# Four edits where the up projection hands over to the down projection: order of small loads, PSUM reads, DRAM copies and late operands

## The chip, the cores and the metric

The kernel runs on one core of a Trainium2 chip. The metric is device time: microseconds of one execution on that core, as the median over several executions. TensorE does the matrix products, VectorE and ScalarE the elementwise work, SyncE issues most of the DMA transfers, ScalarE a few, and GpSimd the DMA transfers that accumulate in DRAM.

## The reference, cut to what matters

One residual block on a sequence of 512 rows with D_MODEL = 2048 and D_FF = 5632, all in float32. The change lies in the second half, from `h2` on, and in one of the six vectors of `mod`, `gt2`.

```python
mod = silu(c) @ w_ada + b_ada                      # (1, 6*2048)
sh1, sc1, gt1, sh2, sc2, gt2 = split(mod, 6)
h = modulate(rms_norm(x, g_mix), sh1, sc1)
mix = concat(rms_norm(rglru(h @ w_in[...])), rms_norm(attention(h @ w_in[...])))
x = x + gt1 * (mix @ w_out)                        # called x1 below
h2 = modulate(rms_norm(x, g_ffn), sh2, sc2)
gate, up = split(h2 @ w_up, 2)                     # each (512, 5632)
x = x + gt2 * ((silu(gate) * up) @ w_down)         # w_down: (5632, 2048)
```

## The kernel before, in words

Every float32 operand is split into a high and a low part, and each product is three TensorE products (high by high, high by low, low by high). ScalarE writes the high part (L221, L228) and VectorE subtracts it from the operand for the low part (L222, L229). In the trace's names `h` and `l` at the end of a tile's name are these parts.

**The up projection.** Its 44 feature tiles of 128 features come one after another (`for f in range(2 * STD, FT)`); the first four are done plainly, the 40 others (f = 4 to 43) by a scheme with seven half-size products in place of eight. Each of the 40 takes two weight chunks `uq_0r` and `uq_1r` of 1 MB (`fast_chunk`, L1025 to L1050): VectorE forms sums of blocks in place (L1043, L1044, L1047), and seven pairs of parts with the endings `a`, `c`, `s` and `t` come out. The two chunks lie in the buffers with the tags "raw" (chunk 0) and "raw2" (chunk 1). The results of a tile stand in four PSUM banks `uf{f}p`. VectorE and ScalarE read them in six instructions, L1079 to L1084, into `ug`, `uu` and `uw`; L1085 and L1086 make silu(gate) * up, and `keep_act` (L955 to L968) forms the sums that the down projection needs and writes them to DRAM as `td`.

**The down projection** has four phases (`PHASES`), again with seven products of blocks: 4 and 5, then 1 and 7, then 6, then 2 and 3. Each phase runs over 11 weight chunks q. A chunk (`dn_chunk`) loads `dq_{q}r` of 1 MB per product, through the same "raw" and "raw2" buffers, loads the activation parts `dq_{q}tl` from `td` (L1108), splits them (L1109, L1110), and splits the weights. The second product of phase 0 adds the first weights to its own (L1115). Two of the phases read weight sums from DRAM, `s2d` and `s4d`; these sums are built during the up projection by `sums24`: two copies of 1 MB on SyncE's queue, then accumulating DMA transfers on GpSimd's queue (L976).

**The vector gt2** is a dot product of `silu(c)` with 2048 columns of `w_ada`. It is formed during the up projection in 64 pieces, one per chunk from the 16th chunk on (`GT2_AT`): a load of 256 KB issued by ScalarE's queue (L173) and one VectorE instruction that multiplies and sums (L183). The 64 pieces share two buffers. After the last piece four small additions make `mod` (L187 to L189), and `gt2_spread` writes `mod` to DRAM as `gt2d` (L1145, on SyncE's queue) and reads it back spread over all partitions as `gt2b` (L1149). `gt2b` and `x1` are operands of the last step, `finish` (L1152).

**What sets the order.** A scheduler orders each engine's instructions by priority, which is the place in the program unless `tc.high_priority(offset=...)` raises it: weight loads and splits by AHEAD = 2000, some PSUM reads by EVAC = 2500. `tc.issue_after` holds a transfer back until a named instruction has been issued. Each engine then runs its list strictly in order. Its transfers are issued in the order of that list, too.

Of the kernel before, what the change touches and what calls it, by code (L numbers as in the profile page):

```python
# [10 lines left out]
AF = mybir.ActivationFunctionType  # L11
# [6 lines left out]
KT = D // P  # L18
# [5 lines left out]
FT = DFF // P  # L24
# [14 lines left out]
EVAC = 2500  # L39
# [25 lines left out]
def block_kernel(ctx, tc, xT, crow, adaT, vecs, bfr, w1, wyr, wqkv0, wqkv, wgate, wout, wup0, wups, wdn, outT):  # L65
    nc = tc.nc
# [32 lines left out]
    with tc.high_priority(offset=100000):  # L99
# [6 lines left out]
        for q in (2, 3):  # L106
            cs = slice(q * 512, (q + 1) * 512)
# [62 lines left out]
    def gt2_load(n):  # L170
        t = cp.tile([P, S], F32, name=f"gt2_{n}", tag="ssq", bufs=2)
        with tc.issue_after(tail_hi[-1]):
            nc.scalar.dma_start(out=t, in_=adaT[GT2 * KT + n // 4, :, (n % 4) * S:(n % 4 + 1) * S])  # L173
        gt2_src[n] = t

    def gt2_piece(n):
        if n == 0:
            gt2_load(0)
        if n < 4 * KT - 1:
            gt2_load(n + 1)  # L180
        t = gt2_src.pop(n)
        r = n % 4
        nc.vector.scalar_tensor_tensor(out=t, in0=t, scalar=1.0, in1=c_b[:, r * S:(r + 1) * S], op0=ALU.mult, op1=ALU.mult,  # L183
                                       accum_out=gt2_acc[:, r, n // 4:n // 4 + 1])
        if n == 4 * KT - 1:
            m = mods[GT2]
            nc.vector.tensor_add(m, gt2_acc[:, 0, :], vec[:, V_BADA + GT2 * KT:V_BADA + (GT2 + 1) * KT])  # L187
            for r in range(1, 4):
                nc.vector.tensor_add(m, m, gt2_acc[:, r, :])  # L189
# [175 lines left out]
    for kt in range(KT):  # L365
        if kt < 2:
            with tc.high_priority(offset=90000):
                xt, raws = w1_loads(kt)
        else:
            xt, raws = w1_loads(kt)  # L370
        a = cp.tile([P, 1], F32, name=f"A{kt}")
# [10 lines left out]
        for i in range(2):  # L382
            cs = slice(i * 512, (i + 1) * 512)
# [594 lines left out]
    def sums24(q, n):  # L978
        if n == 0:
            with tc.issue_after(up_loads[-1]):  # L980
                nc.sync.dma_start(out=s2d[q], in_=wdn[0, q])
                nc.sync.dma_start(out=s4d[q], in_=wdn[1, q])
        elif n < 3:
            dram_sum(s2d[q], wdn[n + 1, q])
        else:
            dram_sum(s4d[q], s2d[q])
# [69 lines left out]
    for f in range(2 * STD, FT):  # L1056
# [19 lines left out]
        w1_, w2_ = (ap_.tile([P, S], F32, tag="x", name=f"uw{f}_{i}", bufs=2) for i in range(2))  # L1076
        two = lambda t: t.rearrange("p (a b) -> p a b", a=2)
        twice = lambda t: t.unsqueeze(1).broadcast_to(halves)
        nc.scalar.activation(w1_[:, lo_half], m[1], AF.Copy)  # L1079
        nc.vector.tensor_add(two(g), two(ps[0]), twice(w1_[:, lo_half]))  # L1080
        nc.vector.tensor_sub(two(w2_), twice(g[:, hi_half]), two(ps[1]))
        nc.vector.tensor_add(g[:, hi_half], m[3], w2_[:, lo_half])  # L1082
        nc.vector.tensor_sub(u[:, lo_half], m[4], w2_[:, hi_half])
        nc.vector.tensor_sub(u[:, hi_half], m[5], w2_[:, hi_half])  # L1084
# [66 lines left out]

    def finish(y, tt, a, nm, out=True):  # L1152
        xt = page(nm + "x", "d")
        nc.sync.dma_start(out=xt, in_=x1t[tt, a])
        nc.vector.tensor_mul(y, y, gt2b[a])
        nc.vector.tensor_add(y, y, xt)
        if out:
            nc.gpsimd.dma_start(out=outT[tt][:, a * S:(a + 1) * S], in_=y)
# [125 lines left out]
```

## Time and profile before

| quantity | value |
|---|---|
| time, median of 3 executions | 2105.34 us (2105.25 to 2111.82) |
| the profiled execution | 2106.22 us, of which its span is 2104.5 us |
| granted TensorE clock, mean of the span | 0.993 |
| TensorE busy | 2046.4 us, 97% of the span |
| VectorE busy | 1707.3 us, 81% |
| ScalarE busy | 942.3 us, 45% |
| GpSimd busy | 92.2 us, 4% |

The span runs from the first to the last recorded activity; 1.72 us lie around it. Busy means that an instruction of that engine was running; the issuing of transfers isn't counted. In the trace a row with `[8.47 <-DVE ug L1080]` tells that the engine stood idle for 8.47 us just before the row, and that the VectorE instruction of line 1080 which wrote `ug` released it. PE is TensorE, DVE VectorE, ACT ScalarE, POOL GpSimd; SPq and ACTq are the transfers that SyncE and ScalarE issue. Granted clock is the share of full TensorE speed that the throttle gave in a stretch.

By time the kernel is: the first input product from 10 to 200 us, attention and the recurrent group to 600, the output projection to 760, the first four feature tiles to 850, the 40 tiles of the fast scheme to 1660.8 (20.2 us each), and the down phases to 1795, 1915, 1964 and 2100 us.

### The profile page before, as it was taken

To read this page: it belongs to the slowest core of one execution; us is meant where nothing else is said; L and a number is where in the kernel's file an instruction comes from. 1 tells how busy PE (TensorE), PEld (TensorE's weight loads), DVE (VectorE), ACT (ScalarE), POOL (GpSimd) and SP (SyncE) were. 2 spreads that over 40 slices of the span, in tenths; PEclk is the share of its full clock that TensorE was granted. 3 is DMA by queue.
4 is the path that set the end of the run, shared out by engine and by line. 5 is a ranking of instruction groups with operands and counts; after the bars stand their busy time and mean duration, and the time that the engine had idled before them with its cause. 6 is when DMAs were issued, how large, how long until landed. Compare 5 with 4: busy or idle time off the path is not lost.

```text
span 2104.5 us, 32286 instructions
## 1 busy us (share of the span) xinstructions
PE 2046.4 (97%) x12529; PEld 1856.7 (88%) x12529; DVE 1707.3 (81%) x2547; ACT 942.3 (45%) x1331; POOL 92.2 (4%) x111
## 2 busy tenths in 40 slices
PE   8999999999999999999999999999999899999999
PEld 6889898888788887999999999999999778888877
DVE  8999768887785569988798888888888777776785
ACT  4433447765433355444343333344434345545443
POOL 0000000100100000000000000000000000000000
PEclk9999999999999999999999999999999999999999
DMA  9989866667677532438877878888877677677784
GB/s 336 345 292 315 254 204 220 221 214 253 231 243 264 182 129 92 132 130 236 226 228 229 237 216 256 250 245 235 240 232 208 188 254 250 233 243 252 260 298 148
DMA packets 168412, 485.21 MB, mean 231 GB/s; under 512 B 20033, under 2 KB 45025, under 8 KB 163810
## 3 DMA queue, kind: packets, MB, share of 16 engines
q1 hardware_dynamic: 148898, 429.66, 59.9%
q0 software_dynamic: 10144, 36.70, 9.7%
q10 hardware_dynamic: 9216, 16.78, 2.4%
q8 instruction: 98, 1.61, 0.3%
q14 instruction: 56, 0.46, 0.1%
HBM read 447.40 MB, written 93.35 MB: 257 GB/s over the span
## 4 chain that ended last, share of the span: by engine, by line
PE 74%; DVE 12%; DMA 9%; issue 2%; ACT 2%; POOL 1%; SPq 0%; DVEq 0%; ACTq 0%
PE w1p L233 4%; PE dn7p L233 3%; PE dn1p L233 3%; DMA gt<-in_adaT 2%; PE dn5p L233 2%; PE dn6p L233 2%; PE yr1p L233 2%; PE up0p L233 2%; PE wo2p L233 2%; PE wo3p L233 2%; PE wo1p L233 2%; PE dn4p L233 2%; PE yr0p L233 2%; PE wo0p L233 2%; PE h3p L233 2%
## 5 line engine op out<-in xcount | busy, mean ns | idle before, releaser
L154 DVE SCALAR_TENSOR_TENSOR ada<-ada,c_b 128x1024 f32<-128x1024 f32 x96 | 116.0, 1219 | 26.8 <-DMA ada<-in_adaT 26.7
L228 ACT ACTIVATE uq_0sh<-uq_0r 128x1024 fp32r<-128x1024 f32 x40 | 42.4, 1060 | 208.3 <-DVE uq_0r L1044 183.6
L183 DVE SCALAR_TENSOR_TENSOR gt<-gt,c_b 128x512 f32<-128x512 f32 x64 | 43.9, 686 | 60.5 <-DMA gt<-in_adaT 60.5
L228 ACT ACTIVATE uq_1sh<-uq_1r 128x1024 fp32r<-128x1024 f32 x40 | 42.5, 1061 | 109.2 <-DVE uq_1r L1044 98.0
L976 POOL DMA_DIRECT2D s2d<-in_wdn x44 | 36.7, 909 | 685.0 <-DMA s2d<-in_wdn 676.8
L228 ACT ACTIVATE uq_0ah<-uq_0r 128x1024 fp32r<-128x1024 f32 x40 | 42.3, 1058 | 48.2 <-DMA td<-tw 3.6
L229 DVE TENSOR_TENSOR uq_0sl<-uq_0r,uq_0sh 128x1024 fp32r<-128x1024 f32 x40 | 49.0, 1226 | 18.1 <-ACT uq_0sh L228 18.1
L229 DVE TENSOR_TENSOR uq_0tl<-uq_0r,uq_0th 128x1024 fp32r<-128x1024 f32 x40 | 48.8, 1220 | 8.4 <-ACT uq_0th L228 8.4
L229 DVE TENSOR_TENSOR uq_0al<-uq_0r,uq_0ah 128x1024 fp32r<-128x1024 f32 x40 | 48.8, 1221 | 8.4 <-ACT uq_0ah L228 8.3
L233 PE MATMUL w1p<-hph,w1h 128*128 128x512 f32 x128 | 47.5, 400 | 6.1 <-ACT hph L377 6.1
L228 ACT ACTIVATE uq_1ah<-uq_1r 128x1024 fp32r<-128x1024 f32 x40 | 42.3, 1057 | 22.4 <-issue 11.9
L233 PE MATMUL w1p<-hpl,w1h 128*128 128x512 f32 x128 | 51.2, 400 | 0.0
L233 PE MATMUL w1p<-hph,w1l 128*128 128x512 f32 x128 | 50.8, 397 | 0.0
L229 DVE TENSOR_TENSOR uq_1tl<-uq_1r,uq_1th 128x1024 fp32r<-128x1024 f32 x40 | 48.8, 1219 | 2.0 <-ACT uq_1th L228 2.0
L1085 ACT ACTIVATE ug<-ug 128x512 f32<-128x512 f32 x40 | 25.3, 633 | 53.5 <-DVE ug L1082 53.5
L1043 DVE TENSOR_TENSOR uq_0r<-uq_0r 128x1024 f32<-128x1024 f32 x40 | 48.7, 1217 | 0.0
L229 DVE TENSOR_TENSOR uq_1sl<-uq_1r,uq_1sh 128x1024 fp32r<-128x1024 f32 x40 | 48.7, 1217 | 0.0
L229 DVE TENSOR_TENSOR uq_1al<-uq_1r,uq_1ah 128x1024 fp32r<-128x1024 f32 x40 | 48.6, 1215 | 0.0
L1043 DVE TENSOR_TENSOR uq_1r<-uq_1r 128x1024 f32<-128x1024 f32 x40 | 48.6, 1214 | 0.0
L228 ACT ACTIVATE uq_0th<-uq_0r 128x1024 fp32r<-128x1024 f32 x40 | 41.9, 1048 | 12.4 <-DVE uq_0r L1047 2.6
L228 ACT ACTIVATE uq_1th<-uq_1r 128x1024 fp32r<-128x1024 f32 x40 | 42.0, 1051 | 10.5 <-PE uf36p L1066 1.3
L164 DVE SCALAR_TENSOR_TENSOR ada<-ada,c_b 128x1024 f32<-128x1024 f32 x32 | 39.0, 1220 | 1.7 <-DMA ada<-in_adaT 1.7
(12770 smaller groups left out, 8149.0 us busy)
## 6 DMA issues: line engine op xcount, KB each, us to landing
ada<-in_adaT SPq DMA_DIRECT2D x128, 512.0 KB, 5.1
uq_1r<-in_wups SPq DMA_DIRECT2D x80, 512.0 KB, 7.5
uq_0r<-in_wups SPq DMA_DIRECT2D x80, 512.0 KB, 5.0
s2d<-in_wdn POOLq DMA_DIRECT2D x44, 512.0 KB, 9.3
adf<-in_adaT SPq DMA_DIRECT2D x32, 512.0 KB, 6.0
gt<-in_adaT ACTq DMA_DIRECT2D x64, 256.0 KB, 4.7
s4d<-s2d POOLq DMA_DIRECT2D x22, 512.0 KB, 9.2
x<-in_xT SPq DMA_DIRECT2D x32, 256.0 KB, 5.6
```

The lines of the kernel that those rows point to most:

```text
L154: nc.vector.scalar_tensor_tensor(out=t, in0=t, scalar=1.0, in1=cs, op0=ALU.mult, op1=ALU.mult, accum_out=ac)
L164: nc.vector.scalar_tensor_tensor(out=t, in0=t, scalar=1.0, in1=c_b[:, cs], op0=ALU.mult, op1=ALU.mult, accum_out=ada_acc[j][:, hf, i:i + 1])
L183: nc.vector.scalar_tensor_tensor(out=t, in0=t, scalar=1.0, in1=c_b[:, r * S:(r + 1) * S], op0=ALU.mult, op1=ALU.mult, accum_out=gt2_acc[:, ...
L228: tail_hi.append(nc.scalar.activation(R(hi[:, :n]), raw_ap, AF.Copy).ins)
L229: tail_lo.append(nc.vector.tensor_sub(R(lo[:, :n]), raw_ap, hi[:, :n]).ins)
L233: nc.tensor.matmul(ps, lhsT=R(l), rhs=R(r), start=start, stop=stop)
L976: nc.gpsimd.dma_start(out=out[:, cs], in_=src[:, cs], accum_op=ALU.add)
L1043: nc.vector.tensor_add(blocks[:, 0:3:2], blocks[:, 0:2], blocks[:, 2:3].broadcast_to([P, 2, 512]))
L1085: nc.scalar.activation(g, g, AF.Silu)
```

## The change

There are four edits.

1. `gt2_piece`: pieces 0 and 1 are loaded at the start, and piece n+2 is loaded after piece n's VectorE instruction; before, piece n+1 was loaded ahead of piece n's instruction. There are still two buffers.
2. `sums24`: each of the two 1 MB copies from DRAM to DRAM is cut in two, over the columns, so that a row of a copy is 1024 floats; there are four transfers per weight chunk instead of two.
3. The six PSUM reads of a feature tile stand in a `high_priority` block, with the offset EVAC for the last tile (f = 43) and 0 for the others.
4. `finish`: its load of `x1` is held back until the last load but one that has been noted in `dn_loads`, the list of down weight loads, has been issued.

```diff
     def gt2_piece(n):
         if n == 0:
             gt2_load(0)
-        if n < 4 * KT - 1:
-            gt2_load(n + 1)
+            gt2_load(1)
         t = gt2_src.pop(n)
         r = n % 4
         nc.vector.scalar_tensor_tensor(out=t, in0=t, scalar=1.0, in1=c_b[:, r * S:(r + 1) * S], op0=ALU.mult, op1=ALU.mult,
                                        accum_out=gt2_acc[:, r, n // 4:n // 4 + 1])
+        if n < 4 * KT - 2:
+            gt2_load(n + 2)
...
             with tc.issue_after(up_loads[-1]):
-                nc.sync.dma_start(out=s2d[q], in_=wdn[0, q])
-                nc.sync.dma_start(out=s4d[q], in_=wdn[1, q])
+                for i in range(2):
+                    cs = slice(i * 1024, (i + 1) * 1024)
+                    nc.sync.dma_start(out=s2d[q][:, cs], in_=wdn[0, q, :, cs])
+                    nc.sync.dma_start(out=s4d[q][:, cs], in_=wdn[1, q, :, cs])
...
-        nc.scalar.activation(w1_[:, lo_half], m[1], AF.Copy)
-        nc.vector.tensor_add(two(g), two(ps[0]), twice(w1_[:, lo_half]))
...
+        with tc.high_priority(offset=EVAC if f == FT - 1 else 0):
+            nc.scalar.activation(w1_[:, lo_half], m[1], AF.Copy)
+            nc.vector.tensor_add(two(g), two(ps[0]), twice(w1_[:, lo_half]))
...
-            nc.sync.dma_start(out=raw[:, i * 1024:(i + 1) * 1024], in_=src[:, i * 1024:(i + 1) * 1024])
+            ld = nc.sync.dma_start(out=raw[:, i * 1024:(i + 1) * 1024], in_=src[:, i * 1024:(i + 1) * 1024])
+        dn_loads.append(ld.ins)
...
         xt = page(nm + "x", "d")
-        nc.sync.dma_start(out=xt, in_=x1t[tt, a])
+        with tc.issue_after(dn_loads[-2]):
+            nc.sync.dma_start(out=xt, in_=x1t[tt, a])
```

The rows of TensorE and GpSimd stand as before but for one swapped pair of matmuls. On the other engines the lists change at three places that the prediction speaks of. In the rows below a number behind a name tells one buffer or piece from another; the line numbers of the changed kernel are some higher than those of the kernel before.

VectorE, from the end of the last up tile into the first down chunk. `uf43p` are the PSUM banks of the last up tile, `dq_0` is the first down chunk. Before:

```order
L229 TENSOR_TENSOR uq_1tl<-uq_1r,uq_1th 128x1024
L1110 TENSOR_TENSOR dq_0tl<-dq_0tl,dq_0th 128x512
L183 SCALAR_TENSOR_TENSOR gt_63_17107,gt_acc<-gt_63_17107,c_b 128x512
L189 TENSOR_TENSOR mod_127<-mod_127,gt_acc 128x16
L229 TENSOR_TENSOR dq_0w0l<-dq_0r,dq_0w0h 128x1024
L1110 TENSOR_TENSOR dq_1tl<-dq_1tl,dq_1th 128x512
L1115 TENSOR_TENSOR dq_1r<-dq_1r 128x2048
L229 TENSOR_TENSOR dq_0w1l<-dq_0r,dq_0w1h 128x1024
L1110 TENSOR_TENSOR dq_1tl<-dq_1tl,dq_1th 128x512
L229 TENSOR_TENSOR dq_0w0l<-dq_0r,dq_0w0h 128x1024
L1110 TENSOR_TENSOR dq_2tl<-dq_2tl,dq_2th 128x512
L1080 TENSOR_TENSOR ug_17221<-uf43p_16997,uw_0_17223 128x512
```

With the change:

```order
L230 TENSOR_TENSOR uq_1tl<-uq_1r,uq_1th 128x1024
L1117 TENSOR_TENSOR dq_0tl<-dq_0tl,dq_0th 128x512
L230 TENSOR_TENSOR dq_0w0l<-dq_0r,dq_0w0h 128x1024
L1117 TENSOR_TENSOR dq_1tl<-dq_1tl,dq_1th 128x512
L1122 TENSOR_TENSOR dq_1r<-dq_1r 128x2048
L230 TENSOR_TENSOR dq_0w1l<-dq_0r,dq_0w1h 128x1024
L1117 TENSOR_TENSOR dq_1tl<-dq_1tl,dq_1th 128x512
L1084 TENSOR_TENSOR ug_17243<-uf43p_17021,uw_0_17245 128x512
L230 TENSOR_TENSOR dq_0w0l<-dq_0r,dq_0w0h 128x1024
L1085 TENSOR_TENSOR uw_1_17246<-ug_17243,uf43p_17022 128x512
L1117 TENSOR_TENSOR dq_2tl<-dq_2tl,dq_2th 128x512
L1086 TENSOR_TENSOR ug_17243<-uf43p_17023,uw_1_17246 128x256
```

The first read of the last tile's banks (`ug`, L1080, now L1084) has moved ahead of the second `dq_0w0l` and of the first `dq_2tl`. Piece 63 of gt2 and the last addition to `mod` have left this stretch: they now stand some twenty rows earlier, behind `uq_1tl` of tile 42 and ahead of `uq_0al` of tile 43.

SyncE's queue over the same stretch. Before:

```order
L1108 DMA dq_0tl<-td_0_6717 128x512
L1154 DMA f210x<-x1t_0_6572 128x512
L1096 DMA dq_1r<-in_wdn 128x1024 x2
L1108 DMA dq_0tl<-td_0_6717 128x512
L1154 DMA f220x<-x1t_2_6592 128x512
L965 DMA td_10_6738<-ug_16985 128x256
L1108 DMA dq_1tl<-td_1_6718 128x512
L1096 DMA dq_1r<-in_wdn 128x1024 x2
L1108 DMA dq_1tl<-td_1_6718 128x512
L1145 DMA gt2d<-mod_127 128x16x1
L1154 DMA f120x<-x1t_2_5960 128x512
L1154 DMA f110x<-x1t_0_5940 128x512
```

With the change:

```order
L1152 DMA gt2d<-mod_127 128x16x1
L1115 DMA dq_0tl<-td_0_6717 128x512
L1100 DMA dq_1r<-in_wdn 128x1024 x2
L1115 DMA dq_0tl<-td_0_6717 128x512
L1115 DMA dq_1tl<-td_1_6718 128x512
L966 DMA td_10_6738<-ug_17009 128x256
L1100 DMA dq_1r<-in_wdn 128x1024 x2
L1115 DMA dq_1tl<-td_1_6718 128x512
L1115 DMA dq_2tl<-td_2_6719 128x512
L1100 DMA dq_2r<-in_wdn 128x1024 x2
```

The transfer `gt2d` now stands ahead of the first `dq_0tl`; it stood behind the second `dq_1tl`. The four loads of `x1` with the names `f210x`, `f220x`, `f120x` and `f110x` are gone from here: they now stand near the end of the third phase, around `dq_10r<-s2d` and ahead of `dq_0r<-s4d`. The twelve other loads of `x1` stand where they stood.

ScalarE in feature tile 13, where the early pieces of gt2 are loaded. Before:

```order
L228 ACTIVATE uq_1th<-uq_1r 128x1024
L228 ACTIVATE uq_0ah<-uq_0r 128x1024
L173 DMA gt_2_9715<-in_adaT 128x512
L1040 ACTIVATE uq_1ch<-uq_1r 128x512
L228 ACTIVATE uq_0sh<-uq_0r 128x1024
```

With the change:

```order
L229 ACTIVATE uq_1th<-uq_1r 128x1024
L173 DMA gt_2_9609<-in_adaT 128x512
L229 ACTIVATE uq_0ah<-uq_0r 128x1024
L173 DMA gt_3_9720<-in_adaT 128x512
L1043 ACTIVATE uq_1ch<-uq_1r 128x512
```

Each load stands one place earlier, and so does its use on VectorE: piece 2 was used between `uq_0r` (L1043) and `uq_0r` (L1044), and is now used between the second and the third of these additions; piece 3 is now used two rows later, ahead of `uq_0tl`. From there on the same two places take turns to the end: a load behind `uq_0th` is used behind `uq_1sl` or `uq_1tl`, a load behind `uq_1th` is used behind `uq_1tl`, in both kernels, with the piece's number one higher in the changed one.

More of the change, by code (lines that the diff above doesn't have):

```diff
@@ L1078, in block_kernel @@
         twice = lambda t: t.unsqueeze(1).broadcast_to(halves)
-        nc.scalar.activation(w1_[:, lo_half], m[1], AF.Copy)
[L1080 to L1084, printed above, removed]
+        with tc.high_priority(offset=EVAC if f == FT - 1 else 0):
+            nc.scalar.activation(w1_[:, lo_half], m[1], AF.Copy)
+            nc.vector.tensor_add(two(g), two(ps[0]), twice(w1_[:, lo_half]))
+            nc.vector.tensor_sub(two(w2_), twice(g[:, hi_half]), two(ps[1]))
+            nc.vector.tensor_add(g[:, hi_half], m[3], w2_[:, lo_half])
+            nc.vector.tensor_sub(u[:, lo_half], m[4], w2_[:, hi_half])
+            nc.vector.tensor_sub(u[:, hi_half], m[5], w2_[:, hi_half])
         nc.scalar.activation(g, g, AF.Silu)
@@ L1095, in dn_load @@
         for i in range(2):
-            nc.sync.dma_start(out=raw[:, i * 1024:(i + 1) * 1024], in_=src[:, i * 1024:(i + 1) * 1024])
+            ld = nc.sync.dma_start(out=raw[:, i * 1024:(i + 1) * 1024], in_=src[:, i * 1024:(i + 1) * 1024])
+        dn_loads.append(ld.ins)
         return raw
+    dn_loads = []
     def dn_chunk(ph, q, hold=False):
```

## The prediction

> **What bounds the kernel now.** I read the busy times first, then what TensorE waits for, then the stretch with the longest wait.
>
> ```profile
> PE 2046.4 (97%) x12529; PEld 1856.7 (88%) x12529; DVE 1707.3 (81%) x2547; ACT 942.3 (45%) x1331; POOL 92.2 (4%) x111
> PE dn5p L233 <- DVE ug L1080: 8.5, 1, 8.5
> ```
>
> TensorE is busy for all but 58.1 us of 2104.5, and none of its matmuls goes away. So an edit can gain only where TensorE waits. The second line, from the view of waits, names the largest single wait of the last third: the first product of `dn5p` waits for the VectorE read of the last up tile's banks. TensorE's own rows give the place, and the chain of work says what was late there:
>
> ```profile
> 1675.87 0.76 PE L233 MATMUL dn5p<-dq_0w0h,dq_0th 128*128 128x512 f32 x1 [8.47 <-DVE ug L1080]
> 1678.06 0.77 PE L233 MATMUL dn5p<-dq_0w0h,dq_0th 128*128 128x512 f32 x1 [0.57 <-DVE ug L1082]
> ...
> 1641.10 19.70 PE uf43p L1066 x164
> 1661.80 11.94 DMA dq_2tl<-td
> 1674.43 0.69 DVE dq_2tl L1110
> 1675.12 0.61 DVE ug L1080
> 1678.06 6.47 PE dn5p L233 x21
> 1684.53 5.45 PE dn4p L233 x24
> ```
>
> The banks were full at 1660.79 (1641.10 plus 19.70). `ug` came at 1675.12 because it stands on VectorE behind `dq_2tl`, which waited for a load that took 11.94 us. The first chunk of `dn4p` and `dn5p` would take twice 5.45 us, to 1671.7, and ended at 1684.53: 12.8 us are lost here. Why the load was slow stands in the view of windows (here the last two columns, the busy share of the DMA engines and GB/s) and in the DMA table (KB and median us to landing):
>
> ```profile
> 1655.00:1660.00 5.00, 5.00 (x44) 5.00 (x43) 2.60 (x6) 1.78 (x3) 0.00 (x0) 1.00 0.92 270
> 1660.00:1665.00 5.00, 4.66 (x26) 3.74 (x25) 3.43 (x2) 0.00 (x0) 0.00 (x0) 1.00 0.52 14
> 1665.00:1670.00 5.00, 2.40 (x10) 1.60 (x9) 1.92 (x2) 1.85 (x3) 0.00 (x0) 1.00 0.60 35
> ...
> gt2d<-mod SPq DMA_DIRECT2D x1, 8.0 KB, 14.1
> f120x<-x1t SPq DMA_DIRECT2D x1, 256.0 KB, 15.4
> f110x<-x1t SPq DMA_DIRECT2D x1, 256.0 KB, 11.7
> dq_1r<-in_wdn SPq DMA_DIRECT2D x4, 512.0 KB, 4.9
> ```
>
> For 10 us the engines are more than half busy and move 14 to 35 GB/s. The one transfer of that shape in flight is `gt2d`: 2048 single floats, 8 KB, 14.1 us. Its issue and those behind it:
>
> ```profile
> 1643.89 0.33 SPq L1108 DMA_DIRECT2D dq_0tl<-td  x1
> 1655.92 0.38 SPq L1145 DMA_DIRECT2D gt2d<-mod  x1
> 1656.40 4.60 SPq L1154 DMA_DIRECT2D f120x<-x1t  x1
> 1661.42 0.32 SPq L1154 DMA_DIRECT2D f110x<-x1t  x1
> ```
>
> `gt2d` landed at 1670.0; `f110x`, issued 5.5 us behind it, at 1673.1, and `dq_2tl` at 1673.7. Whatever is issued behind `gt2d` lands some 3.1 to 3.7 us after it.
>
> **The handover with the change.** Two edits meet here. The PSUM reads no longer stand behind `dq_2tl`, and `gt2d` moves. In VectorE's new order the last addition to `mod` stands where this row stood, so `gt2d` is issued at about 1639, 17 us earlier, and directly ahead of the first `dq_0tl`, whose issue (1643.89) waits for TensorE to free its page and doesn't move. The slow stretch therefore goes from 1660 back to 1639. What it now holds up is in these VectorE and ScalarE rows:
>
> ```profile
> 1638.68 0.16 DVE L189 TENSOR_TENSOR mod<-mod,gt_acc 128x16 f32<-128x16 f32 x1
> 1649.38 0.69 DVE L1110 TENSOR_TENSOR dq_0tl<-dq_0tl,dq_0th 128x512 fp32r<-128x512 f32 x1
> 1652.12 1.22 DVE L229 TENSOR_TENSOR uq_1sl<-uq_1r,uq_1sh 128x1024 fp32r<-128x1024 f32 x1
> 1653.25 1.22 DVE L229 TENSOR_TENSOR uq_1tl<-uq_1r,uq_1th 128x1024 fp32r<-128x1024 f32 x1
> 1661.32 2.29 DVE L1115 TENSOR_TENSOR dq_1r<-dq_1r 128x2048 f32<-128x2048 f32 x1 [3.69 <-DMA dq_1r<-in_wdn]
> ...
> 1647.44 0.61 ACT L1109 ACTIVATE dq_0th<-dq_0tl 128x512 fp32r<-128x512 f32 x1
> ```
>
> Call T the landing of that `dq_0tl`. On ScalarE `dq_0th` stands ahead of `uq_1sh`, on VectorE `dq_0tl` ahead of `uq_1sl`, which TensorE needs for tile 43. From T to the end of `uq_1sl` it is 0.61 for `dq_0th` and the 3.96 from 1649.38 to 1653.34, so T + 4.6. TensorE needs it at 1655.3: the second chunk of the tile starts 84 matmuls of 0.12 us before 1660.79, and the pair stands 38 matmuls behind that. So TensorE stalls by T less 1650.7.
>
> T follows from how long `gt2d` alone blocks: at least the 10 us of the slow windows (to 1649), at most its 14.1 us (to 1653.1) with the 3.1 us behind (1656.2). I take the middle, T = 1652.6, since 1.35 MB (270 GB/s for 5 us) still went ahead of `gt2d` before and little does now. Then:
>
> - tile 43 ends 1.9 us late, at 1662.7; `uq_1tl` ends at T + 6.3 (with 0.6 for the `ug` now between the two) = 1658.9 and frees the buffer of `dq_1r`;
> - `dq_1r` lands 4.9 us later, 1663.8; the addition takes 2.29, `dq_0w1l` 1.22, so 1667.3; the second half of `dn4p` waits 1.9 us for it and ends at 1670.0;
> - behind it on VectorE `dq_1tl` 0.69, `ug` 0.69, `dq_0w0l` 1.22, `uw` 0.69, `dq_2tl` 0.69, three short reads of 0.42: the last bank is free at 1672.5. `dn5p` begins at 1670 to 1672.5 and, with 5.45 us, ends at 1677.9 at the latest.
>
> Against 1684.53 that gains **6.6 us**. Each us of T moves the end by one, so for T of 1649 and 1656.2 the gain is 10.2 and 3.0.
>
> **The pieces of gt2.** The 64 uses of a piece leave VectorE idle for 60.5 us:
>
> ```profile
> L183 DVE SCALAR_TENSOR_TENSOR gt<-gt,c_b 128x512 f32<-128x512 f32 x64 | 43.9, 686 | 60.5 <-DMA gt<-in_adaT 60.5
> 1017.10 0.34 ACTq L173 DMA_DIRECT2D gt<-in_adaT  x1
> 1028.78 0.69 DVE L183 SCALAR_TENSOR_TENSOR gt<-gt,c_b 128x512 f32<-128x512 f32 x1 [7.89 <-DMA gt<-in_adaT]
> 1031.31 0.39 PE L1066 MATMUL uf13p<-td0h,uq_0sh 128*128 128x256 f32 x1 [3.08 <-ACT uq_0sh L228]
> 1032.57 0.58 PE L1066 MATMUL uf13p<-td0h,uq_0sl 128*128 128x256 f32 x1 [0.76 <-DVE uq_0sl L229]
> ```
>
> In the new lists load and use both move one place up, so the time from issue to use stays what it was from piece 4 on, and I cost those at nothing either way. Piece 2 stopped TensorE longest: 3.84 us in these rows. Now it is issued some 2.2 us earlier (behind `uq_1th` instead of `uq_0ah`), and `uq_0sh` no longer stands behind its use, but piece 3 is used two rows later. Between 1.3 us and all 3.84, I take **2.0**.
>
> **The copies in short rows.** Their size stays 1 MB; the queue gets 22 transfers more. The rows nearest to a price are the waits for a gt2 piece, once beside the copies and once beside the accumulating sums of GpSimd:
>
> ```profile
> 1086.36 0.69 DVE L183 SCALAR_TENSOR_TENSOR gt<-gt,c_b 128x512 f32<-128x512 f32 x1 [2.32 <-DMA gt<-in_adaT]
> 1109.54 0.69 DVE L183 SCALAR_TENSOR_TENSOR gt<-gt,c_b 128x512 f32<-128x512 f32 x1 [3.97 <-DMA gt<-in_adaT]
> 1111.44 0.39 PE L1066 MATMUL uf17p<-te0h,uq_0al 128*128 128x256 f32 x1 [0.80 <-DVE uq_0al L229]
> ...
> PE uf41p L1066 <- DVE uq_0al L229: 1.3, 1, 1.3
> ```
>
> Only the second, beside the sums, reaches TensorE (0.80 us), and the sums are as before. So nothing, between a gain of 4.8 us (TensorE's eight groups of waits in the fast tiles beside those of `uf13p`, of which the last row is the longest) and the loss under the rivals.
>
> **The late loads of x1.** They now stand around the last load of the third phase, `dq_10r<-s2d`, and add 1 MB to these two windows:
>
> ```profile
> 1940.00:1950.00 10.00, 10.00 (x46) 8.29 (x45) 5.87 (x7) 4.73 (x6) 0.00 (x0) 1.00 0.69 224
> 1950.00:1960.00 10.00, 10.00 (x46) 8.28 (x45) 5.58 (x6) 4.96 (x6) 0.00 (x0) 1.00 0.75 255
> 1985.64 0.68 DVE L1156 TENSOR_TENSOR q<-q,f210x 128x512 f32<-128x512 f32 x1
> 2048.07 0.73 PE L233 MATMUL dn3p<-dq_6w0h,dq_6th 128*128 128x512 f32 x2 [1.40 <-ACT dq_6w0h L228]
> ```
>
> At 240 GB/s these are 4.4 us of transfer; the engines are free for 3.1 plus 2.5 us of these windows, and `finish` first reads `x1` at 1985.64, 30 us later. If the cover fails, the weight loads behind come up to 4.4 us late, in a phase in which TensorE already waits at 2048. I take **0.5 us** lost, between 0 and 4.4. The reorder inside the other feature tiles (offset 0) adds no instruction and moves reads by a row or two; nothing.
>
> **The sum.** 6.6 + 2.0 - 0.5 = 8.1 us. The profiled execution (2106.22, span 2104.5) lies 0.9 over the median, so I take it off the median: 2105.3 - 8.1 = **2097.2 us**. With the bounds of the handover and the smaller terms the forecast's own range is 2092 to 2101.
>
> **The rivals.**
>
> - *A: the slow transfer is covered in its new place.* Between 1640 and 1645 little else is in flight; were `gt2d` done in 8 us, T would not bind. Then `uq_1tl` ends at about 1655.1 with the `ug` between, the chain above runs 3.8 us earlier, and the end is 1674.1: 10.4 + 2.0 - 0.5, 2093.4 us. Against it stand the 10 us of the slow windows. [...]
> - *B: the slow transfer is only moved.* T = 1656.2, TensorE stalls 5.5 us inside tile 43 and gains 3.0 behind it: 2105.3 - 4.5 = 2100.8. For it: `f120x`, issued right behind `gt2d`, took 15.4 us.
> - *C: short rows free the gt2 loads.* If long rows of a copy hold up another queue's packets, halving the waits beside the copies lets VectorE catch up before the sums, and up to 4.8 us of TensorE waits go: 2092.4. The row at 1086.36 speaks a little for it, the longer wait at 1109.54 against it. [...]
> - *D, the other side: short rows make the copies cost more.* Each has 256 rows instead of 16; if they hold the loads of a gt2 piece or of `uq` longer, each of the 11 cycles ends in one more TensorE wait. At the longest seen behind a late piece (1.3 us in `uf41p`), 14.3 us are lost: 2111.5. It decides once a cycle loses 0.8 us, as then the 8.1 are gone. Against it: no TensorE wait stands beside the copies now.
>
> **How the numbers follow.** Forecast 0.45, A 0.15, B 0.20, C 0.10, D 0.10. I call 0.3%, 6.3 us, what a measurement tells from no change. A, C and three quarters of the forecast gain more: faster 0.58. B and the rest of the forecast: same 0.32. D, with some late loads of x1 on top: slower 0.10. The range 2089 to 2107 leaves out most of D and a little below A and C together.
>
> **What would show it.** `gt2d` issued near 1639 with a landing of 10 to 14 us, and 14 to 35 GB/s just behind; a wait of TensorE of 0 to 5.5 us inside `uf43p` near 1655, ended by `uq_1sh` or `uq_1sl`; no wait over 3 us before `dn5p`, and full clock there; the 3.08 us at `uf13p` gone or under 1.5; VectorE's idle before L182 still near 60 us. I am wrong if `gt2d` lands in under 8 us, if `dq_0tl` lands ahead of it, if new waits stand in the cycles of the copies, or if TensorE waits more than 4 us longer from 1964 on.

## The result, and the profile after

| | before | with the change | ratio, 95% interval |
|---|---|---|---|
| median | 2111.06 us (6 executions, 2105.25 to 2117.17) | 2098.54 us (6, 2093.93 to 2101.16) | 0.9943 [0.992, 0.9965] |
| once more, beside other kernels | 2106.28 us (35) | 2098.82 us (12, 2095.26 to 2107.61) | 0.9968 [0.9946, 0.9989] |
| profiled execution, its span | 2106.22 us, 2104.5 us | 2100.19 us, 2098.5 us | |

The change makes the kernel faster by 12.0 us by the first comparison (7.4 to 16.9) and by 6.7 us by the second (2.3 to 11.4). The forecast was 8.1 us and 2097.2 us. The changed kernel stood at nearly the same time both times; it is the kernel before that stood 5 us higher in the first comparison than in the later ones (2105.5 to 2106.3 us), so the 12.0 is the less certain of the two gains.

To see where the time went, the two traces are cut at four matmuls: the first of tile 4, the first of tile 43, the first of `dn1p`, the first of `dn6p`. (`uf43p` is the tile's name in the rows, `dn1p` and `dn6p` begin the second and the third down phase.) The stretch from tile 43 to `dn1p` is called the handover; without any wait it would be 139.8 us, an estimate from the traces (84 + 84 matmuls of 0.12 us, and 22 times 5.44 us, which is the 119.68 us from `dn1p` to `dn6p` by 22).

| stretch | before | with the change | difference |
|---|---|---|---|
| start to tile 4 | 833.84 | 836.32 | +2.5 |
| tile 4 to tile 43 | 807.09 | 807.18 | +0.1 |
| handover | 154.15 | 146.65 | -7.5 |
| `dn1p` to `dn6p` | 119.68 | 119.68 | 0.0 |
| `dn6p` to the end of the span | 189.77 | 188.63 | -1.1 |

Up to tile 4 the change alters nothing. In the profiles of all the kernels told of here the first matmul of tile 4 lies anywhere between 832.1 and 837.5 us. So a single total says little about a few us, and the stretches are compared instead. They vary too: among the profiles of kernels with the same fast tiles as the changed one, tile 4 to tile 43 took 806.4 to 812.0 us.

**The handover.** TensorE's rows with a wait, with the change, from tile 43 to `dn1p`:

```profile
1659.60 0.39 PE L1069 MATMUL uf43p<-td4h,uq_1sh 128*128 128x256 f32 x1 [1.54 <-ACT uq_1sh L229]
1660.86 0.58 PE L1069 MATMUL uf43p<-td4h,uq_1sl 128*128 128x256 f32 x1 [0.76 <-DVE uq_1sl L230]
1674.95 0.47 PE L234 MATMUL dn5p<-dq_0w0h,dq_0th 128*128 128x512 f32 x1 [1.18 <-DVE ug L1086]
1697.43 0.73 PE L234 MATMUL dn5p<-dq_2w0l,dq_2th 128*128 128x512 f32 x2 [0.25 <-DVE dq_2w0l L230]
1708.87 0.74 PE L234 MATMUL dn5p<-dq_3w0l,dq_3th 128*128 128x512 f32 x2 [0.27 <-DVE dq_3w0l L230]
```

The wait of 8.47 us before `dn5p` is 1.18 us now, and two waits stand where there was none, inside tile 43. What is late there is told by SyncE's queue, the chain of work and the windows (last two columns: busy share of the DMA engines, GB/s; the column before them is the granted clock):

```profile
1641.67 0.37 SPq L1152 DMA_DIRECT2D gt2d<-mod  x1
1646.45 0.32 SPq L1115 DMA_DIRECT2D dq_0tl<-td  x1
...
1646.45 9.88 DMA dq_0tl<-td
...
1645.00:1650.00 5.00, 5.00 (x44) 5.00 (x44) 4.90 (x7) 2.01 (x2) 0.00 (x0) 1.00 0.09 2
1650.00:1655.00 5.00, 5.00 (x44) 5.00 (x43) 2.12 (x3) 0.00 (x0) 0.00 (x0) 1.00 0.54 59
1660.00:1665.00 5.00, 4.24 (x24) 4.14 (x24) 4.88 (x6) 2.50 (x5) 0.00 (x0) 0.66 0.36 116
```

Tile 43 began at 1643.50, 2.57 us later than before, so on the clock of the kernel before `gt2d` was issued at 1639.1. Behind it the engines move 2 GB/s for 5 us, and `dq_0tl` takes 9.88 us, where the same load took 3.03 us before (issued at 1643.89, landed at 1646.92). The engines' share is 0.09 in these 5 us: by the profile's count of packets they are hardly busy. Even transfers issued ahead of `gt2d` are held up: two stores to `td`, issued 3.0 and 2.3 us before it, took 7.6 and 8.3 us, and 5.3 and 5.0 us in the kernel without edit 1 below, where `gt2d` comes later. The chain behind it on VectorE, and the first matmul of the second chunk of `dn4p`:

```profile
1659.58 1.22 DVE L230 TENSOR_TENSOR uq_1sl<-uq_1r,uq_1sh 128x1024 fp32r<-128x1024 f32 x1
1661.32 1.22 DVE L230 TENSOR_TENSOR uq_1tl<-uq_1r,uq_1th 128x1024 fp32r<-128x1024 f32 x1
1667.51 2.29 DVE L1122 TENSOR_TENSOR dq_1r<-dq_1r 128x2048 f32<-128x2048 f32 x1 [2.63 <-issue]
1675.05 0.41 DVE L1088 TENSOR_TENSOR uu<-uf43p,uw 128x256 f32<-128x256 f32 x1
...
1680.24 0.62 PE L234 MATMUL dn4p<-dq_1w0h,dq_1th 128*128 128x512 f32 x2
```

The load landed at 1656.33, `uq_1sl` ended 4.5 us and `uq_1tl` 6.2 us after that, `dq_1r` was added 4.9 us behind its issue, and the first chunk ended at 1680.24; less the 2.57 us this is 1677.7.

These are one profile's numbers. In a second profile of the same kernel (told of below) `dq_0tl` took 7.6 us and landed at 1651.5 on the clock of the kernel before, 2.3 us earlier; TensorE waited only 0.28 us inside tile 43, and the first chunk ended at 1675.6 on that clock.

**The up tiles.** The waits of TensorE and the idle of VectorE before a piece of gt2 (the page's row) with the change:

```profile
PE uf26p L1069 <- DVE uq_0al L230: 2.3, 1, 2.3
PE uf20p L1069 <- DVE uq_0al L230: 1.4, 1, 1.4
PE uf14p L1069 <- DVE uq_0al L230: 1.1, 1, 1.1
PE uf32p L1069 <- DVE uq_0al L230: 0.8, 1, 0.8
...
L182 DVE SCALAR_TENSOR_TENSOR gt<-gt,c_b 128x512 f32<-128x512 f32 x64 | 43.9, 685 | 61.3 <-DMA gt<-in_adaT 61.3
```

The wait at `uf13p` is gone, and others have come at `uf14p`, `uf20p` and `uf26p`. The pieces are as late as before: 61.3 us of idle against 60.5, and 20 of the 64 are waited for in both kernels. The stretch from tile 4 to tile 43 has not become shorter.

### The profile page after: what moved, and what is told of

The parts are those of the page before. It is cut to its first block, busy times and chain, and to the rows that moved or that the text cites. A ratio compares the mean times of both kernels' runs of the same rounds, so it can differ in the third digit from the quotient of the medians.

```text
span 2098.5 us, 32298 instructions
## 1 busy us (share of the span) xinstructions
PE 2047.3 (98%) x12529; PEld 1856.8 (88%) x12529; DVE 1709.0 (81%) x2547; ACT 939.6 (45%) x1331; POOL 92.6 (4%) x111
## 4 chain that ended last, share of the span: by engine, by line
PE 73%; DVE 13%; DMA 9%; issue 2%; ACT 2%; POOL 1%; SPq 0%; ACTq 0%; DVEq 0%
PE w1p L234 4%; DMA gt<-in_adaT 3%; PE dn6p L234 3%; PE dn7p L234 3%; PE dn1p L234 3%; PE yr1p L234 2%; PE up0p L234 2%; PE wo2p L234 2%; PE wo1p L234 2%; PE wo3p L234 2%; PE dn3p L234 2%; PE dn5p L234 2%; PE wo0p L234 2%; PE dn2p L234 2%; PE yr0p L234 2%
## 5 line engine op out<-in xcount | busy, mean ns | idle before, releaser
L182 DVE SCALAR_TENSOR_TENSOR gt<-gt,c_b 128x512 f32<-128x512 f32 x64 | 43.9, 685 | 61.3 <-DMA gt<-in_adaT 61.3
```

## The experiments

The theory tested is this: the transfer `gt2d`, 2048 single floats, sets the handover through whichever load stands behind it, and the pieces of gt2 are late in the up tiles in both kernels. The rivals: that the place of the PSUM reads set it (edit 3), that short rows or the late loads of x1 matter, and that the DMA is simply full. Each kernel was timed beside the kernel before; the table gives the ratio with its interval and, from one profile of each, the two stretches that matter. The names in brackets are those that the expectations use.

| kernel | ratio | tile 4 to 43 | handover |
|---|---|---|---|
| before | 1 | 807.1 | 154.2 |
| the change | 0.9943 [0.992, 0.9965] | 807.2 | 146.7 |
| the change, again | 0.9968 [0.9946, 0.9989] | 806.4 | 145.8 |
| without edit 3 (PSUM reads) | 0.9965 [0.9952, 0.9978] | 809.5 | 145.1 |
| without edit 1 (gt2 loads) | 0.9972 [0.9961, 0.9983] | 806.1 | 149.2 |
| without edit 2 (short rows) | 0.9935 [0.9923, 0.9948] | 807.9 | 144.7 |
| without edit 4 (late x1) | 0.9963 [0.9949, 0.9977] | 812.0 | 148.2 |
| the change, gt2d in 64 runs | 0.9966 [0.9945, 0.9987] | 807.6 | 142.0 |
| the change, gt2d on ScalarE's queue | 0.9955 [0.9935, 0.9974] | 809.8 | 147.1 |
| before, gt2d in 64 runs | 0.9958 [0.9937, 0.9979] | 809.6 | 143.4 |
| the change, gt2 used two chunks later (`g_lead`) | 0.9915 [0.9899, 0.993] | 794.7 | 150.7 |
| the same and gt2d in 64 runs (`g_leadtr`) | 0.9874 [0.9859, 0.989] | 794.7 | 140.1 |
| the same without edit 2 | 0.9883 [0.9866, 0.99] | 794.7 | 141.4 |
| before, with gt2 later and in 64 runs | 0.9892 [0.9871, 0.9913] | 794.6 | 144.5 |

### One edit undone at a time

Without edit 3 in the last tile (the block with offset 0 stays in all tiles):

```diff
-        with tc.high_priority(offset=EVAC if f == FT - 1 else 0):
+        with tc.high_priority(offset=0):
```

> The changed kernel with edit 3 undone: the six reads of the last up tile's PSUM banks stand at their old priority (offset 0 for all tiles), so VectorE does the second dq_0w0l and the first dq_2tl ahead of ug again; gt2d stays where the change put it. Measure: the handover, from the first matmul of tile 43 to the first of dn1p (154.3 us before, 146.8 with the change; 139.8 would be without any wait). Theory (the slow transfer gt2d sets the handover, through whichever load stands behind it): dq_2tl is issued well after gt2d has landed, so ug comes some 2 us later than with the change and the handover is 148 to 150; total 1 to 3 us over the changed kernel. Rival (the priority of the PSUM reads carries the gain): the wait of 8.5 us before dn5p is back and the handover is 153 to 155; total 6 to 8 us over the changed kernel.

The handover was 145.1 us, no longer than with the change (146.7 and 145.8) and below the 148 to 150 that the theory expected. `ug` stands behind `dq_2tl` again, and TensorE's wait for it is short:

```profile
1671.12 0.50 PE L234 MATMUL dn5p<-dq_0w0h,dq_0th 128*128 128x512 f32 x1 [0.37 <-DVE ug L1084]
```

With `gt2d` out of the way of `dq_2tl`, it makes no difference that `ug` stands behind that load. The rival is out: by this profile nothing of the 7.5 us needs the raised reads once `gt2d` is early.

Without edit 1:

```diff
-            gt2_load(1)
+        if n < 4 * KT - 1:
+            gt2_load(n + 1)
...
-        if n < 4 * KT - 2:
-            gt2_load(n + 2)
```

> The changed kernel with edit 1 undone: piece n+1 of gt2 is loaded ahead of piece n again, so gt2d is issued near 1656, behind the second dq_1tl, and the PSUM reads stay raised. Theory: the first dq_0tl lands in time and no wait stands in uf43p; the slow transfer now holds up dq_1tl and dq_2tl as before, ug no longer waits for dq_2tl but the three last reads do, so TensorE waits before and in dn5p for 3 to 6 us; handover 148 to 151. At uf13p the wait of 3 to 4 us is back. Total 3 to 8 us over the changed kernel. Rival (moving gt2d cost more than it gained, since TensorE stalls in uf43p because of it): handover 143 to 146, total within 2 us of the changed kernel or under it.

The handover was 149.2 us. No wait stands in `uf43p`; one stands before `dn5p` (TensorE's row, the VectorE row that held up the read, then from the DMA table the load that this row needs):

```profile
1675.78 0.77 PE L233 MATMUL dn5p<-dq_0w0h,dq_0th 128*128 128x512 f32 x1 [5.90 <-DVE ug L1085]
...
1674.61 0.69 DVE L1116 TENSOR_TENSOR dq_2tl<-dq_2tl,dq_2th 128x512 fp32r<-128x512 f32 x1 [3.56 <-ACT dq_2th L1115]
...
dq_2tl<-td SPq DMA_DIRECT2D x1, 256.0 KB, 14.5
```

So with `gt2d` at its old place the other edits gain 5.0 of the 14.4 us that the handover of the kernel before loses against 139.8, and the early `gt2d` gains some 3 us more. The raised reads explain little of the shorter wait: it ends with the third of VectorE's reads (L1085), which still stands behind `dq_2tl`. It is 2.6 us shorter, and `dq_2tl` landed 2.5 us earlier (1671.2 against 1673.7 on the clock of the kernel before), with two loads of x1 no longer in the queue ahead of it. How the 5.0 us divide between edits 3 and 4 is not shown.

One thing was expected wrongly: the wait of 3 us at `uf13p` was not back. That wait for `uq_0sh` stood in the kernel before and in that kernel with the new write of `gt2d` (2.9 us), and in none of the kernels built on the changed one. With edit 1 undone the load of the piece still stands one place earlier in tile 13, so the order there isn't edit 1's work alone. Which of the edits ended the wait stays open, since edits 3 and 4 (of edit 3 the block with offset 0) stand in every kernel that undoes edit 1 or edit 2.

Without edit 2:

```diff
-                for i in range(2):
-                    cs = slice(i * 1024, (i + 1) * 1024)
-                    nc.sync.dma_start(out=s2d[q][:, cs], in_=wdn[0, q, :, cs])
-                    nc.sync.dma_start(out=s4d[q][:, cs], in_=wdn[1, q, :, cs])
+                nc.sync.dma_start(out=s2d[q], in_=wdn[0, q])
+                nc.sync.dma_start(out=s4d[q], in_=wdn[1, q])
```

> The changed kernel with edit 2 undone: the copies from DRAM to DRAM in 16 rows of 64 KB again. Theory: nothing; TensorE's waits in the fast up tiles stay at 6 to 11 us (8.7 before, 8.6 with the change), VectorE's idle before a piece of gt2 at 55 to 67 us, handover 146 to 148, total within 3 us of the changed kernel. Rival C (short rows free the loads of gt2): waits in the up tiles over 12 us, total 4 us or more over. Rival D (short rows make the copies dearer): waits under 5 us, total 4 us or more under.

Tile 4 to 43 took 807.9 us, the handover 144.7. VectorE's idle before a piece was 60.8 us, and TensorE's waits in the fast tiles, without the 2.7 us at the bias products of tile 4, came to 8.9 us against 8.6: neither rival shows in the waits. The total came out lower than with the other edits undone (ratio 0.9935; 5 us under the changed kernel's median, where within 3 was expected), but the stretch with the copies is no shorter; in its profile tile 4 began at 832.1 us against 836.3, ahead of the first copy. A second pair, below, decides.

Without edit 4:

```diff
-        with tc.issue_after(dn_loads[-2]):
-            nc.sync.dma_start(out=xt, in_=x1t[tt, a])
+        nc.sync.dma_start(out=xt, in_=x1t[tt, a])
```

> The changed kernel with edit 4 undone: the four first loads of x1 stand in the handover again, f210x and f220x behind the first two dq_0tl, f120x and f110x ahead of the first dq_2tl. Theory: 1 MB more on the queue behind gt2d, 4.4 us at 240 GB/s, of which the chain over dq_1r and dq_2tl sees a part: handover 147 to 151. From dn6p to the end of dn2p (183.9 us with the change, 185.0 before) 0 to 1 us shorter or the same. Total 0 to 4 us over the changed kernel. Rival (the late loads cost in the last phase): that stretch 2 us or more shorter and the total under the changed kernel.

The handover was 148.2 us, 1.5 to 2.3 us longer than with the change. The longest wait in it comes behind the addition to `dq_1r`:

```profile
1673.16 0.74 PE L234 MATMUL dn4p<-dq_0w1l,dq_0th 128*128 128x512 f32 x2 [3.28 <-DVE dq_0w1l L230]
```

The second half of `dq_1r`, issued 1.2 us ahead of `f120x`, took 6.5 us to land; in the second profile of the changed kernel it took 4.6, and the wait there was 1.36 us. So in the handover the late loads of x1 are worth about as much as was expected, as far as single profiles show it. From `dn6p` to the end it took 187.9 us against 188.6 and 188.5, but other kernels with the late loads took 187.3 to 188.6, so a loss there isn't shown. The totals don't tell the two kernels apart.

### The slow transfer

The changed kernel once more, beside the next three:

> The changed kernel as it is, once more, beside the three variants below on one chip. Theory: ratio to the kernel before 0.993 to 0.998; handover (first matmul of tile 43 to the first of dn1p) 144 to 149 us; TensorE's waits from tile 4 to tile 43 at 10 to 14 us (11.3 in the first profile), VectorE's idle before a piece of gt2 at 55 to 66 us.

The handover was 145.8 us, the waits from tile 4 to 43 came to 10.3 us and the idle before the pieces to 54.9. Here the trace has the landing of `gt2d`, and TensorE's only wait inside tile 43:

```profile
gt2d<-mod SPq DMA_DIRECT2D x1, 8.0 KB, 11.0
...
1656.55 0.39 PE L1069 MATMUL uf43p<-td4h,uq_1sl 128*128 128x256 f32 x1 [0.28 <-DVE uq_1sl L230]
```

Its write in 64 runs of 128 bytes:

```diff
-        nc.sync.dma_start(out=gd.rearrange("k p -> p k"), in_=mods[GT2])
+        g32, t32 = (cp.tile([P, 32], F32, name=f"gt2s{i}") for i in range(2))
+        nc.vector.memset(g32, 0.0)
+        nc.vector.tensor_copy(out=g32[:, :KT], in_=mods[GT2])
+        nc.vector.transpose(out=t32, in_=g32)
+        for b in range(4):
+            nc.sync.dma_start(out=gd[:, b * 32:(b + 1) * 32], in_=t32[b * 32:b * 32 + KT, :])
```

> The changed kernel, but gt2d is written in 64 runs of 128 bytes instead of 2048 single floats: mod is copied into a 128x32 tile, VectorE transposes its 32x32 blocks, and four transfers of 16 rows write it. Theory (the 2048 single elements make the slow stretch): no stretch below 100 GB/s while loads are waiting, dq_0tl lands within 6 us of its issue, no wait in uf43p; handover 141 to 144 us, total 1 to 6 us under the changed kernel. Rival (the loads of the handover are late because 1.3 MB each wait for one another, whatever gt2d does): handover 145 us or more, and dq_0tl still over 8 us.

The DMA table of the handover (KB, us to landing) and two windows of it:

```profile
dq_0tl<-td SPq DMA_DIRECT2D x2, 256.0 KB, 4.0
gt2d<-gt2s SPq DMA_DIRECT2D x4, 2.0 KB, 4.3
dq_2tl<-td SPq DMA_DIRECT2D x1, 256.0 KB, 3.4
...
1645.00:1650.00 5.00, 5.00 (x44) 5.00 (x44) 4.98 (x8) 2.50 (x3) 0.00 (x0) 1.00 0.16 56
1650.00:1655.00 5.00, 5.00 (x44) 5.00 (x43) 5.00 (x9) 2.13 (x4) 0.00 (x0) 1.00 0.81 276
```

`dq_0tl` lands in 4.0 us at the median of two, the slow stretch is gone (in the first row little but one `dq_0tl` was asked for), and no wait stands in `uf43p`. The handover is 142.0 us. But the edit moved the transfer too: with the two VectorE instructions added it is issued behind the second `dq_1tl`, no longer ahead of `dq_0tl`. So `dq_0tl` tells nothing of the new shape here. The load now behind the transfer does: `dq_2tl` took 3.4 us, and 14.5 us behind the single floats at the same place in the kernel without edit 1, whose handover was 149.2. The median is 2.0 us under that of the changed kernel beside it, which the intervals don't tell apart. The pair further below, in the kernel before, changes the shape and leaves the place.

The same transfer of single floats on the other queue:

```diff
-        nc.sync.dma_start(out=gd.rearrange("k p -> p k"), in_=mods[GT2])
+        nc.scalar.dma_start(out=gd.rearrange("k p -> p k"), in_=mods[GT2])
```

> The changed kernel, but the one transfer gt2d is issued by ScalarE's queue instead of SyncE's, still as 2048 single floats. If what blocks is the order within SyncE's queue, dq_0tl and what follows land within 6 us and the handover is 141 to 144 us. If the elements take the DMA engines themselves, or completions wait for them across the queues, it stays at 145 to 149 us with a landing of dq_0tl over 8 us. I hold the first for a little likelier (0.55).

```profile
gt2d<-mod ACTq DMA_DIRECT2D x1, 8.0 KB, 10.9
...
dq_0tl<-td SPq DMA_DIRECT2D x2, 256.0 KB, 9.2
...
1645.00:1650.00 5.00, 5.00 (x44) 5.00 (x43) 4.89 (x8) 2.01 (x2) 0.00 (x0) 1.00 0.07 9
```

The first expectation fell. On ScalarE's queue `gt2d` takes as long (10.9 us against 11.0), `dq_0tl` on SyncE's queue, issued 4.8 us after it, is as late (9.2 us at the median of two), and the handover is 147.1 us. What blocks is not the order within one queue: the elements sent by ScalarE's queue hold up a load on SyncE's. The data itself came late: the engines moved 9 GB/s from 1645 to 1650 (last row), and 56 in that stretch with the 64 runs. What exactly the elements hold up is not shown.

The write in 64 runs alone, in the kernel before:

> The kernel before with nothing changed but the write of gt2d, in 64 runs of 128 bytes as described for the changed kernel; ug stays behind dq_2tl on VectorE. Theory: dq_2tl lands within 7 us, the wait of 8.5 us before dn5p falls under 2.5 us, handover 142 to 147 us against 154.2; total 7 to 12 us under the kernel before, as much as all four edits together. Rival (the place of the PSUM reads behind dq_2tl is the cause, whatever the load takes): handover 150 us or more.

TensorE's wait before `dn5p`, the two VectorE rows that had made it, and the load:

```profile
1672.80 0.47 PE L233 MATMUL dn5p<-dq_0w0h,dq_0th 128*128 128x512 f32 x1 [1.32 <-DVE ug L1082]
...
1669.17 0.69 DVE L1110 TENSOR_TENSOR dq_2tl<-dq_2tl,dq_2th 128x512 fp32r<-128x512 f32 x1
1669.77 0.69 DVE L1080 TENSOR_TENSOR ug<-uf43p,uw 128x512 f32<-128x512 f32 x1
...
dq_2tl<-td SPq DMA_DIRECT2D x1, 256.0 KB, 2.8
```

`ug` still stands behind `dq_2tl`, but `dq_2tl` no longer waits: its load, behind `gt2d` as before, took 2.8 us instead of 11.9. The handover is 143.4 us, 10.8 us shorter, by that one write; all four edits together shortened it by 7.5 (8.3 in the second profile). The order of the reads was only the way in which the slow transfer reached TensorE.

### The late pieces of gt2

The diff against the changed kernel (`tail_lo` lists the last splits of the weight chunks so far):

```diff
-        nc.vector.scalar_tensor_tensor(out=t, in0=t, scalar=1.0, ...
+        with tc.issue_after(tail_lo[-1]):
+            nc.vector.scalar_tensor_tensor(out=t, in0=t, scalar=1.0, ...
```

> The changed kernel, and the VectorE instruction of a gt2 piece is held back until the last split of its own weight chunk has been issued, so that a piece is used two chunks (some 20 us) after its load instead of right behind it. gt2d moves back to where the kernel before had it, behind the second dq_1tl. Theory (in both kernels the pieces are late because they are used at once, and that alone makes TensorE's waits in the fast tiles): VectorE's idle before a piece falls from 61 us to under 10, the sum of TensorE's waits from tile 4 to tile 43 from 10 to 14 us to 3 to 5 (2.7 of it are the bias products of tile 4). The handover is that of the kernel with edit 1 undone, 148 to 151 us (149.2 there). Total 1 to 6 us under the changed kernel. Rival (the pieces are late because the DMA engines are full at those times): the idle stays over 30 us and the waits over 8.

The page's row for the pieces, a load and the piece's use, and TensorE's wait in the handover:

```profile
L183 DVE SCALAR_TENSOR_TENSOR gt<-gt,c_b 128x512 f32<-128x512 f32 x64 | 43.6, 683 | 0.0
...
1097.81 0.33 ACTq L173 DMA_DIRECT2D gt<-in_adaT  x1
1116.42 0.68 DVE L183 SCALAR_TENSOR_TENSOR gt<-gt,c_b 128x512 f32<-128x512 f32 x1
...
1661.90 0.77 PE L235 MATMUL dn5p<-dq_0w0h,dq_0th 128*128 128x512 f32 x1 [7.53 <-DVE ug L1087]
```

The piece shown is used 18.6 us behind its load (in the kernel before: 8.7 us for the piece used at 1109.54, with a wait of 3.97), and not one is late. At the median it is 19.4 us, and 10.8 with the change. So the DMA was not simply too full for these loads, and that rival is out. TensorE's waits from tile 4 to 43 fall from 11.3 to 2.9 us, and the stretch from 807.2 to 794.7. The handover is 150.7 us, as with edit 1 undone, since `gt2d` is back behind `dq_1tl`. The median is 11 us under those of the changed kernel, not 1 to 6. The two were not timed side by side, though: by the ratios to the kernel before it is 6 to 11 us, and by the two stretches 7 to 8, so the total is at least at the upper end of what was expected. The stretch became 12.5 us shorter where the waits in it fell by 8.4; why is told under the last heading.

Both together:

> The kernel of g_lead with the write of gt2d in 64 runs of 128 bytes. Theory: the two effects add up. TensorE's waits from tile 4 to tile 43 are 3 to 5 us, the handover is 141 to 144 us; the total is 8 to 14 us under the changed kernel, a ratio to the kernel before of 0.990 to 0.993. Rival (one takes the place of the other, or the freed VectorE time runs into the sums and copies): waits over 7 us or handover over 145, total within 6 us of the changed kernel.

The medians stand at 2079.40 us against 2106.15 us, a ratio of 0.9874 [0.9859, 0.989]: faster than both kernels. This is the largest TensorE wait left in the fast tiles beside the 2.7 us at the bias products of tile 4, from the view of waits:

```profile
PE uf4p L1070 <- DVE uq_1sl L231: 0.2, 1, 0.2
```

From tile 43 to `dn1p` no TensorE row has a wait at all. The effects add up; the total is 19 us under the changed kernel by the medians and 14.5 to 19.8 by the ratios, more than the 8 to 14 expected, mostly by the up tiles. Against the kernel with only the late use, the write in 64 runs shortens the handover by 10.6 us.

The same with rows of 64 KB, the diff of edit 2 undone as above:

> The kernel of g_leadtr with edit 2 undone: the copies from DRAM to DRAM in rows of 64 KB again. The kernel with edit 2 undone had a ratio of 0.9935 against 0.9943 and 0.9968 for the changed one, which may be chance. If the rows matter in themselves, the total is 3 us or more under g_leadtr, with shorter landings of uq_1r (6.7 to 7 us median against 8 to 9) that end in fewer waits. If they don't, both are within 3 us, and TensorE's waits from tile 4 to 43 are the same within 2 us.

2079.73 us against 2079.40 us, and the same 794.7 us from tile 4 to 43. The rows make no difference that these runs can show; the lower total with edit 2 undone was not repeated.

And the two causes alone, in the kernel before (the new loads with the held back use, and the 64 runs, without edits 2, 3 and 4):

> The kernel before with two things only: the loads of gt2 and the held back VectorE instruction as in g_lead, and the write of gt2d in 64 runs of 128 bytes. Edits 2, 3 and 4 are not in it. If these three add nothing beside the two causes, TensorE's waits from tile 4 to tile 43 are under 4 us, the handover is 140 to 144 us (140.1 in g_leadtr) and the ratio to the kernel before is 0.986 to 0.990, as in g_leadtr (0.9874). If the raised PSUM reads or the late loads of x1 still matter, the handover is 145 us or more and the ratio over 0.990. Here ug stands behind two dq_2tl, so I give the second 0.35.

A ratio of 0.9892 [0.9871, 0.9913], no different from the 0.9874 within the intervals. The handover was 144.5 us against 140.1, with four waits of 0.3 to 1.5 us; `ug` stands behind two `dq_2tl` there. So edits 3 and 4 may keep some 4 us in the handover once the causes are gone; by one profile each this is not settled, and the totals don't show it.

## Why the prediction was right

*What bounds the kernel.* Right in the place and the cause: the wait of 8.47 us came from `gt2d` by way of `dq_2tl`. The kernel before with only the write changed shows it. One reading was too wide: not all that is issued behind `gt2d` lands 3.1 to 3.7 us after it, `f120x` landed 1.8 us after it.

*Where `gt2d` goes.* Forecast 1639, measured 1639.1 on the clock of the kernel before. *How late `dq_0tl` is.* T was forecast as 1652.6, between 1649 and 1656.2; measured 1656.33 less 2.57, 1653.8, and 1651.5 in the second profile. The middle was a choice between two bounds, and that it fits so well is in part luck. *The wait in tile 43.* Forecast 1.9 us (and 3.1 by the formula for the measured T), measured 1.54 + 0.76 in two waits; the tile took 24.3 us instead of 20.2, because the clock fell after them (0.53 from 1661 to 1664), which the forecast left out. In the second profile the wait was 0.28 us, where the formula gives 0.8. *The end of the first chunk.* Forecast 1677.9, measured 1677.7. Two errors cancel in it: every link up to `dq_0w1l` came 1.1 us later than written (1668.4 against 1667.3), and the end is 1.4 us earlier than the formula gives for the measured T, since `dn5p` began at 1670.8 and waited only 1.2 us for the banks; the second profile gives 1.2 us earlier. *The gain of the handover.* 6.6 us forecast, 7.5 measured (8.3 in the second profile). It was forecast at the end of the first chunk, where 6.7 to 8.8 us were gained. The 11.0 us that `gt2d` takes there lies between the two bounds that were taken for it, 10 and 14.1 us.

*The pieces of gt2.* That load and use move together, and so nothing is gained from piece 4 on, was right: 61.3 us of idle. The term that was mis-sized is the gain of **2.0 us** at piece 2. The wait at `uf13p` did go, and tile 13 became 5.4 us shorter (26.0 to 20.6), more than its waits of 3.84, but the stretch measured +0.1 us. The same lateness fell on other tiles, 1.1 us at `uf14p`, 1.4 at `uf20p`, 2.3 at `uf26p`. Since the stretch varies by 5.6 us between profiles, a gain of 2.0 could hardly have been seen in it at all. A wait that moves with the chance meeting of loads and sums should have been costed over the whole stage and not at the one place where it was seen.

*The short rows.* Nothing was forecast, and the pair with and without them shows nothing in the total. *The late loads of x1.* 0.5 us lost was forecast for the last stretch. Between the profiles with and without edit 4 it is 0.6 to 0.7 us longer with the late loads, which is less than the spread among kernels that have them (187.3 to 188.6), so the term is neither confirmed nor refuted. What their absence gains in the handover, 1.5 to 2.3 us by the same profiles, lay unnamed in the 6.6 us, whose chain was worked out without them.

*The rivals.* A (covered in its new place) is out: `gt2d` took 11.0 us, not 8, and a wait stands in `uf43p` in both profiles. B (only moved) is out by its price: T was 2.4 and 4.7 us under its bound; the totals alone would not exclude it. C (short rows free the pieces) is out: the idle before the pieces stayed at 61.3 us, and with long rows it was 60.8. D (dearer copies) is out: with late use and the new write, long and short rows give the same 794.7 us. That the sum came out close owes something to chance: the 2.0 us of the pieces did not come, while the handover gave 0.9 us more than forecast and the last stretch, where 0.5 us were to be lost, came out 1.1 us shorter, which no run puts down to an edit.

## What to carry to other kernels

A transfer of 8 KB in single floats cost this kernel 10.8 us: ask of every load that is late what small scattered transfer is in flight beside it, on any queue, before moving work around it. Loading a buffer earlier gained nothing here, because the scheduler moved the use up with it; the distance from load to use is what counts, and here it had to be held open from the side of the use. A wait that a profile shows at one place in a periodic stage is a sample: cost it over the stage.

## What the runs showed that was not expected

The waits in the trace understate here what a late operand costs. With the change, tiles 13 to 42 took 13.9 us longer than with the late use (1.5 us of that are gained back in tile 4, which no piece touches, hence the 12.5), and the rows show 8.4 of it. Part is in how rows count: in the kernel before, the wait of 0.80 us at 1111.44 lies between matmuls that start at 1110.36 and 1111.44, where 0.12 us would have passed, so 0.96 us were lost, and the next one started 0.22 us later. That is 0.26 us beyond the row at this wait; for the 13 such waits with the change it makes 3.4 us, an estimate from this one. Part is the clock (the number before the last two, in windows of the changed kernel):

```profile
1046.00:1052.00 6.00, 4.86 (x38) 4.66 (x39) 5.45 (x7) 2.65 (x4) 0.00 (x0) 1.00 0.76 219
1295.00:1298.00 3.00, 2.69 (x12) 2.69 (x13) 2.93 (x5) 0.16 (x1) 0.00 (x0) 0.53 0.29 71
1661.00:1664.00 3.00, 3.00 (x15) 3.00 (x16) 3.00 (x4) 1.48 (x3) 0.00 (x0) 0.53 0.27 83
```

The wait of 1.08 us at `uf14p` (first row) left the clock at 1.00. The one of 2.35 us at `uf26p`, and the 1.54 and 0.76 us close together in `uf43p`, were each followed by some 3 us at 0.53, in which a matmul started every 0.21 us instead of 0.12: about 1.2 us more for each, an estimate from these starts. So one wait of 2.35 us was enough. From tile 4 on, in the first profiles of the kernel before and of the changed one, five waits were of 2.35 to 8.47 us, and the clock fell to 0.50 or 0.51 by 2 us after the end of each (in that of 8.47 us within the wait). The six single waits of 1.03 to 1.40 us left it at 1.00. Two that lay close together in the kernel before, 1.40 us at 2048.07 and 0.53 at 2049.33, were followed by 0.50. Ahead of tile 4, waits of 2.36 us (822.76, before) and 2.99 us (825.31, with the change) left it at 1.00. The length of a wait alone doesn't decide.
